# Gate modulation moved into block 0's attention, a third convolution tap per unit there, more on ScalarE, and 12 gate weights stored one block later

## The chip, the core and the metric

The kernel runs on one NeuronCore of a Trainium2 chip. Five engines have queues of their own: TensorE (PE in the profile; its weight loads are PEld), VectorE (DVE), ScalarE (ACT), GpSimd (POOL) and SyncE (SP, which here only issues DMAs). Each engine works through its queue in order. The metric is the device time of one execution in microseconds; lower is better.

## What is computed

One inference step of a streaming encoder layer, over 2048 prompt frames and 32 sample frames of width 1024, all in float32:

```python
mod = c @ w_mod + b_mod                       # shift, scale, gate: 3 x 1024
h = rms_norm(x, g_pre) * (1 + scale) + shift
z = h @ w_in                                  # 5632 columns: a b z_conv q k v z_attn g_conv g_attn
u = a * sigmoid(b)
y = causal_depthwise_conv(u, width 31) + dw_b
y_conv = (silu(layer_norm(y)) * silu(z_conv)) @ w_conv_out
o = band_attention(q, k, v, bias)             # own 64-frame chunk and the 8 before it, 8 heads
y_attn = (o * silu(z_attn)) @ w_attn_out
merged = sigmoid(g_conv) * y_conv + sigmoid(g_attn) * y_attn
y = x + gate * rms_norm(merged @ w_o, g_post)
```

## The kernel before

A float32 operand is split in two parts, `hi` (rounded to the matmul's float32r) and `lo` (the remainder); a product takes three matmuls, hi·hi, hi·lo and lo·hi (`mm3`). The work goes in four blocks of 512 prompt frames; block 0 also has the 32 sample frames, so its streams are 544 wide and its projections run as two matmuls of 272 columns where the other blocks run one of 512.

A block has these stages. The **attention**: the v projection, then 24 (block 0) or 16 units of scores, softmax, transposes and value products, with the projections of q, k, a, b, z between them as filler, in the order that `FILL` names. The **gate stage**: 16 gate projections (`C_GC`, `C_GA`; matmul tile `pj`, evacuated by ACT into `t`) with the attention branch's output product (`py<-ah`) after every fourth; a DVE instruction `t<-t,py` evacuates that. The **conv-out stage**: 8 steps of 24 matmuls `py<-cohi,w` and `py<-colo,w`, each step led by four transposes `pxt` of the next block's input, which `h_part` scales (`hh`, `hf`) and splits. Then the **output stage** with `w_o`, the post-norm and the stores.

The convolution is 31 taps for each of four channel tiles, 124 DVE instructions `y<-u,dww,y` a block. They are put between other work: in attention by `pace.pump(TP[i])` at three places in a unit, elsewhere wherever the planner `Pace`, which counts TensorE and VectorE time as it writes the program, finds DVE behind. When all taps are done, `norm_conv` follows (POOL sums, two means by matmul `pmean`, `rsqrt` on DVE) and then `co`, which makes `cohi` and `colo`; the conv-out stage needs all four channel tiles of them.

A weight of 0.5 MB is loaded by SP into one of two buffers `raw` (`w_load`, four weights ahead of its use), copied by ACT and subtracted by DVE or POOL into one of three buffers `w` (`w_parts`, two ahead); in block 0 ACT then issues a 1 MB store of both halves (`w_keep`, one ahead). Later blocks load the stored halves (`w<-kept`) and split nothing. In block 0's gate stage (`pace.dense`) every split is DVE's. The eight weights of the gate's modulation (`mod`) are used there too, in `gate_rows`: four pairs of four matmuls `pm` for each half of the row, then `pg`, two DVE instructions and a store of the row to DRAM.

Every engine's order but SP's is the order in which the program is written. Matmul results live in three PSUM tiles of the tag `pp` (`pj`, `py`, `pm`, `pg`, `pmean`, `pxt`): a new one waits until the engine that evacuates the third last is through.

## Time and profile before

| | |
|---|---|
| three timed runs | median 1776.56 us (1776.23 to 1776.82) |
| the profiled execution | 1774.66 us, of it span 1772.9 us |
| mean granted TensorE clock | 0.982 |
| PE busy | 1690.7 us (95%) |
| PEld busy | 1430.4 us (81%) |
| DVE busy | 1154.7 us (65%) |
| ACT busy | 597.5 us (34%) |
| POOL busy | 212.1 us (12%) |
| DMA | 368.61 MB, mean 208 GB/s |

The span is from the first instruction to the last; the profiled execution's own time has 1.76 us more around it. An engine that is busy all along can still be slow, and a busy share is a mean over stages with different limits, so the stages have to be read one by one. In the rows below, a time in brackets is how long the engine sat idle before the instruction, with the instruction that ended the wait.

### The profile page before, as it was taken

Reading aid. Unit: us, or ns where it says so; the run is one execution under the profiler, and the core shown is the slowest. Engines: PE = TensorE matmul, PEld = TensorE weight load, DVE = VectorE, ACT = ScalarE, POOL = GpSimd, SP = SyncE. Lnnn points to the kernel's source line nnn. Section 1 sums busy time; section 2 is a strip of 40 time slices with the busy share of each in tenths; the row PEclk is TensorE's granted clock in tenths of the full one; section 3 lists DMA queues with packets and bytes.
Section 4 is the critical chain, followed back from the end, with each engine's and each line's share of the span. In section 5 each row is a group of like instructions: output and inputs, shape, how many; then the busy total and the mean of one; then the engine's idle time right before and its main releaser. Section 6 shows DMA issues by size and latency. Waiting matters only on the chain.

```text
span 1772.9 us, 23618 instructions
## 1 busy us (share of the span) xinstructions
PE 1690.7 (95%) x9221; PEld 1430.4 (81%) x9221; DVE 1154.7 (65%) x2119; ACT 597.5 (34%) x1156; POOL 212.1 (12%) x163
## 2 busy tenths in 40 slices
PE   6889999989499999999899999999999999999997
PEld 4778899988388788888788888888888888888886
DVE  6556876887855957775652967765652967766523
ACT  5345454233331245531220035531320045531211
POOL 4322222002220000001120000001120000000120
PEclk9999999999699999999999999999999999999999
DMA  8796565767375684465465585455565574445553
GB/s 267 216 326 207 189 215 202 272 229 262 132 255 196 243 305 174 156 221 190 150 217 188 196 307 188 140 198 210 181 218 191 199 272 144 171 167 201 190 190 143
DMA packets 132326, 368.61 MB, mean 208 GB/s; under 512 B 9326, under 2 KB 75050, under 8 KB 101975
## 3 DMA queue, kind: packets, MB, share of 16 engines
q1 hardware_dynamic: 123575, 304.19, 50.1%
q10 hardware_dynamic: 8640, 62.92, 8.7%
q8 instruction: 73, 1.20, 0.3%
q14 instruction: 38, 0.31, 0.1%
HBM read 280.41 MB, written 91.77 MB: 210 GB/s over the span
## 4 chain that ended last, share of the span: by engine, by line
PE 78%; DVE 8%; DMA 4%; ACT 2%; issue 1%; ACTq 0%; POOL 0%; DVEq 0%; SPq 0%; POOLq 0%
PE pj L153 44%; PE py L153 8%; PE pv L153 4%; PE sps L153 4%; PE pt L157 4%; PE op L153 3%; PE oT L153 3%; PE oS L153 3%; PE oP L153 1%; DVE y L134 1%; DVE w L134 1%; PE vS L153 1%; PE vT L153 1%; DMA raw<-in_w_attn_out_dram 1%; DMA raw<-in_w_in_dram 1%
## 5 line engine op out<-in xcount | busy, mean ns | idle before, releaser
L153 PE MATMUL pj<-hh,w 128*128 128x512 f32 (+1 forms) x4800 | 974.7, 357 | 11.9 <-DVE kk L134 6.1
L153 PEld LDWEIGHTS pj<-hh,w 128*128 128x128 f32 x4800 | 778.4, 189 | 133.2 <-issue 8.9
L134 DVE SCALAR_TENSOR_TENSOR y<-u,dww,y 128x512 f32<-128x512 f32 (+1 forms) x480 | 338.2, 770 | 0.4
L1073 ACT ACTIVATE sp<-sp,mn 128x640 f32<-128x640 f32 (+5 forms) x136 | 103.7, 762 | 112.5 <-DVE mn L134 112.3
L1108 ACT ACTIVATE pth<-pt 128x256 fp32r<-128x256 f32 (+4 forms) x184 | 91.9, 501 | 135.8 <-PE pt L157 129.3
L134 DVE TENSOR_TENSOR ptl<-pt,pth 128x256 fp32r<-128x256 f32 (+4 forms) x184 | 104.2, 567 | 27.2 <-ACT pth L1108 25.4
L134 DVE CUSTOM_DVE_ANT_0 sp<-sps,bias 128x640 f32<-128x640 f32 (+4 forms) x128 | 94.4, 737 | 29.6 <-PE sps L153 28.1
L153 PE MATMUL py<-cohi,w 128*128 128x512 f32 (+1 forms) x320 | 93.5, 366 | 19.2 <-ACT cohi L1260 17.7
L226 ACT ACTIVATE w<-raw 128x1024 fp32r<-128x1024 f32 x72 | 75.6, 1054 | 89.1 <-DMA raw<-in_w_mod_dram 18.6
L153 PE MATMUL py<-ah,w 128*128 128x512 f32 (+1 forms) x480 | 96.3, 356 | 8.3 <-DVE t L134 7.1
L153 PEld LDWEIGHTS py<-ah,w 128*128 128x128 f32 x480 | 80.1, 192 | 23.5 <-DVE t L134 7.5
L157 PE MATMUL pt<-ident,sp 128*128 128x128 f32 (+1 forms) x600 | 94.2, 272 | 0.0
L228 POOL TENSOR_TENSOR w<-raw,w 128x1024 fp32r<-128x1024 f32 x30 | 73.3, 2443 | 170.5 <-ACT w L226 142.8
L528 POOL TENSOR_TENSOR u<-y 128x512 f32<-128x512 f32 (+1 forms) x4 | 6.3, 1581 | 671.4 <-DVE y L134 671.4
L153 PEld LDWEIGHTS py<-cohi,w 128*128 128x128 f32 x320 | 58.8, 195 | 29.0 <-ACT cohi L1260 19.1
L134 DVE TENSOR_SCALAR sp<-sp,ll 128x640 f32<-128x640 f32 (+5 forms) x136 | 75.6, 556 | 4.8
L134 DVE TENSOR_TENSOR w<-raw,w 128x1024 fp32r<-128x1024 f32 x42 | 53.3, 1278 | 31.5 <-ACT w L226 31.0
L153 PE MATMUL sps<-kk,qh 128*128 128x320 f32 (+1 forms) x224 | 69.2, 316 | 3.3 <-DVE kk L134 2.0
L157 PEld LDWEIGHTS pt<-ident,sp 128*128 128x128 f32 (+1 forms) x600 | 68.8, 140 | 3.9 <-issue 1.3
L153 PE MATMUL sps<-kk,ql 128*128 128x320 f32 (+1 forms) x224 | 70.8, 323 | 0.0
L1344 POOL TENSOR_TENSOR mg<-mg,t 128x512 f32<-128x512 f32 (+1 forms) x32 | 46.4, 1451 | 168.7 <-issue 114.0
L134 DVE SCALAR_TENSOR_TENSOR t<-t,py 128x512 f32<-128x512 f32 (+1 forms) x40 | 23.2, 584 | 59.3 <-PE py L153 59.2
(247 smaller groups left out, 2224.8 us busy)
## 6 DMA issues: line engine op xcount, KB each, us to landing
w<-kept SPq DMA_DIRECT2D x176, 1024.0 KB
kept<-w ACTq DMA_DIRECT2D x60, 1024.0 KB
raw<-in_w_in_dram SPq DMA_DIRECT2D x48, 512.0 KB
bias<-bias_d SPq DMA_DIRECT2D x32, 320.0 KB
xt<-in_x_prompt_dram SPq DMA_DIRECT2D x16, 512.0 KB
wm<-in_w_mod_dram SPq DMA_DIRECT2D x16, 512.0 KB
xr<-in_x_prompt_dram SPq DMA_DIRECT2D x16, 512.0 KB
vs_d<-vcur SPq DMA_DIRECT2D x12, 512.0 KB
```

The source lines that it names most:

```text
L134: return fn(out, *a, **k)
L153: nc.tensor.matmul(out, lhsT=lhsT, rhs=rhs, start=start, stop=stop)
L157: nc.tensor.transpose(out, in_, idn)
L226: act(wh, raw, AF.Copy)
L228: (V if on_v else G).tensor_tensor(wl, raw, wh.bitcast(F32), op=OP.subtract)
L528: G.tensor_tensor(s2[:, 0:YW], Y[2][:, 0:YW], Y[3][:, 0:YW], op=OP.add)
L1073: self.ex[i] = lambda: act(sp[0:m, 0:nk], sp[0:m, 0:nk], AF.Exp, bias=mn[0:m], scale=-1.0, accum_out=ll[0:m])
L1108: act(self.ph[0:r, f0:f1], pt[0:r, o:o + f1 - f0], AF.Copy)
L1344: G.tensor_tensor(mg, mg, t2, op=OP.add)
```

## The change

Seven edits:

1. The modulation's eight weights leave the gate stage. `FILL(0)` gets `m0` to `m7` between the projections of block 0's attention, and `mod_part` takes the place of `gate_rows`: each weight's four matmuls go into a `pp` tile of their own, and the partial sums are added in SBUF (two ACT copies, six DVE additions), in the space of `aof`. In attention the planner gives their split to POOL.
2. `TP` becomes (1, 1, 1): a third tap in each of 21 units of block 0's attention. The fill budget goes from 88 to 95 us.
3. `twice` names 12 gate weights (channels 256 to 1023 of both gates) beside v's: block 0 doesn't store them; block 1 loads them raw, splits them once more on DVE and stores them; blocks 2 and 3 load the halves as before.
4. In `h_part` and in `co`, the instructions `hf` and `xn<-y,vecs` go from DVE to ACT.
5. `rsqrt` has 9 instructions where it had 11 (one step of higher order in place of two), and the factor 1/1024 of the mean goes into the squares.
6. `ql`, which lies in the `raw` buffers, is made anew in blocks 2 and 3, with four POOL memsets each, since block 1 now loads into them.
7. A yield of 1.5 between `pg` and its DVE instructions.

```diff
-TP = (1, 1, 0)
+TP = (1, 1, 1)
...
-    order = "b0 a0 q1 k1 b1 a1 b2 q2 k2 a2 z0 b3 a3 z1 q3 k3 z2 z3 c0 c1 c2 c3" if b == 0 else \
+    order = "b0 a0 q1 m0 k1 m1 b1 m2 a1 m3 b2 q2 m4 k2 m5 a2 m6 z0 m7 b3 a3 z1 q3 k3 z2 z3 c0 c1 c2 c3" if b == 0 else \
...
-                if b == 0 and m + i:
-                    plan.append(mods.pop(0))
...
+    def twice(key):
+        return key[0] == "v" or key[0] == "in" and key[1] >= C_GC + 2 * P and not C_GA <= key[1] < C_GA + 2 * P
-    keep_at = {key: at[1 if key[0] == "v" else 0] for key, at in uses.items()}
+    keep_at = {key: at[1 if twice(key) else 0] for key, at in uses.items()}
...
-                on_v = key[0] == "mod" or pace.dense or pace.idle is None and pace.dve <= pace.pe + DV
+                on_v = pace.dense or key[0] == "in" and i > uses[key][0] or pace.idle is None and pace.dve <= pace.pe + DV
...
-        V.tensor_scalar(xh, x, -0.5, None, op0=OP.mult)
-        for _ in range(iters):
-            V.tensor_tensor(t, y, y, op=OP.mult)
-            V.tensor_tensor(t, t, xh, op=OP.mult)
-            V.scalar_tensor_tensor(y, t, 1.5, y, op0=OP.add, op1=OP.mult)
+        V.scalar_tensor_tensor(t, y, -0.5, y, op0=OP.mult, op1=OP.mult)
+        V.tensor_tensor(t, t, x, op=OP.mult)
+        V.scalar_tensor_tensor(y, t, 1.5, y, op0=OP.add, op1=OP.mult)
+        V.tensor_tensor(t, y, y, op=OP.mult)
+        V.tensor_tensor(t, t, x, op=OP.mult)
+        V.tensor_scalar(u, t, 0.375, -1.25, op0=OP.mult, op1=OP.add)
+        V.tensor_tensor(u, u, t, op=OP.mult)
+        V.scalar_tensor_tensor(y, u, 1.875, y, op0=OP.add, op1=OP.mult)
...
-        V.tensor_scalar(hf, src, Gm[:, w, ct:ct + 1], Sh[:, w, ct:ct + 1], op0=OP.mult, op1=OP.add)
+        act(hf, src, AF.Identity, scale=Gm[:, w, ct:ct + 1], bias=Sh[:, w, ct:ct + 1])
...
+    def mod_part(i):
+        n, kp = i // 4, i % 4
+        m4, bm, gr = aof[0:4, 3, 0:512], aof[0:2, 2, 0:512], aof[0:2, 1, 0:512]
+        if kp == 0:
             nc.sync.dma_start(bm, dram(b_mod, 2 * D + n * 512, [[0, 2], [1, 512]]))
             nc.sync.dma_start(gr, dram(g_post, n * 512, [[0, 2], [1, 512]]))
+        wh, wl = weights(("mod", 2 * kp, (4 + n) * 512))
+        pm = pp_tile("pm")
+        for kk in range(2):
+            mm(pm[0:4], c4[:, 2 * kp + kk, :], wh[:, kk, :], kk == 0, False)
+            mm(pm[0:4], c4[:, 2 * kp + kk, :], wl[:, kk, :], False, kk == 1)
+            yield
+        if kp == 0:
+            act(m4, pm[0:4], AF.Copy)
+        else:
+            V.tensor_tensor(m4, pm[0:4], m4, op=OP.add)
+        if kp == 3:
+            pace.start(gate_row(n, m4, bm, gr), 1.5)
...
-            if b == 1:
+            if b:
+                qls.clear()
...
-            rate = (88.0 if b == 0 else 62.0) / sum(loads)
+            rate = (95.0 if b == 0 else 62.0) / sum(loads)
...
-                        V.tensor_scalar(xn[ct][:, o0:o1], Y[ct][:, a0:a1], vecs[:, 44 + ct:45 + ct],
-                                        vecs[:, 48 + ct:49 + ct], op0=OP.mult, op1=OP.add)
+                        act(xn[ct][:, o0:o1], Y[ct][:, a0:a1], AF.Identity, scale=vecs[:, 44 + ct:45 + ct],
+                            bias=vecs[:, 48 + ct:49 + ct])
```

How the order moves shows at three places. TensorE, block 0, the last third of the gate stage up to the first conv-out step; `pmean` are the means of `norm_conv`, the second pair of rows of each group for the sample columns. Before:

```order
L153 MATMUL pj<-hh,w 128x272 x93
L153 MATMUL pmean<-lnhi,onesr 128x512
L153 MATMUL pmean<-lnlo,onesr 128x512
L153 MATMUL pmean<-lnhi,onesr 128x32
L153 MATMUL pmean<-lnlo,onesr 128x32
L153 MATMUL pj<-hh,w 128x272 x3
L153 MATMUL pm<-w,c_91 4x512 x4
L153 MATMUL py<-ah,w 128x272 x48
L153 MATMUL pm<-w,c_91 4x512 x4
L583 MATMUL pg<-m_4460,sel 2x512
```

After it came the second `pmean` group and then `pxt`. Now:

```order
L155 MATMUL pj<-hh,w 128x272 x45
L155 MATMUL pmean<-lnhi,onesr 128x512
L155 MATMUL pmean<-lnlo,onesr 128x512
L155 MATMUL pmean<-lnhi,onesr 128x32
L155 MATMUL pmean<-lnlo,onesr 128x32
L155 MATMUL pj<-hh,w 128x272 x147
L155 MATMUL py<-ah,w 128x272 x48
L159 MATMUL pxt<-ident,xt 128x128 x4
L155 MATMUL py<-cohi,w 128x272
```

This is the second group: 147 + 48 matmuls now stand between it and the conv-out stage where none stood, and no `pm` or `pg` is left here.

VectorE, block 0's attention, from one sample unit into the next unit (`ISA` are the bias and minimum of the scores, `ptl` the low half of the transposed softmax). Before:

```order
L134 TENSOR_SCALAR sp<-sp,ll 32x544
L134 SCALAR_TENSOR_TENSOR y<-u,dww,y 128x574
L134 TENSOR_TENSOR kk<-pj,kk 64x272 x4
L134 TENSOR_TENSOR vh<-zcb,vh 128x4x128
L134 ISA sp,mn<-sps,bias 128x128
L134 ISA mn 128x1
L134 TENSOR_TENSOR ptl<-pt,pth 128x512
```

Now:

```order
L136 TENSOR_SCALAR sp<-sp,ll 32x544
L136 SCALAR_TENSOR_TENSOR y<-u,dww,y 128x574
L136 TENSOR_TENSOR kk<-pj,kk 64x272 x4
L136 TENSOR_TENSOR vh<-zcb,vh 128x4x128
L136 SCALAR_TENSOR_TENSOR y<-u,dww,y 128x574
L136 TENSOR_TENSOR aof<-pm,aof 4x512
L136 ISA sp,mn<-sps,bias 128x128
L136 ISA mn 128x1
```

A tap and an addition of `pm` have come in ahead of the scores. Over the whole attention the taps go from 42 to 63, and those that are left for the gate stage from 82 to 61.

VectorE, block 1's gate stage, where `t<-t,py` evacuates the second product of the third `py` group (`ss`, `rr`, `rt`, `ru` belong to the statistics of the next block's input, `u` to `norm_conv`'s `rsqrt`). Before:

```order
L134 TENSOR_TENSOR ru<-rr 128x8
L134 TENSOR_TENSOR ru<-ru,rt 128x8
L134 SCALAR_TENSOR_TENSOR rr<-ru,rr 128x8
L134 TENSOR_SCALAR xt<-xt,rr 128x1024 x4
L134 SCALAR_TENSOR_TENSOR t_8066<-t_8066,py 128x512
L134 SCALAR_TENSOR_TENSOR t_8152<-t_8152,py 128x512
L134 TENSOR_SCALAR xn<-y,vecs 128x512
```

Ahead of these stood the 11 instructions on `u`, with no `t` between. Now:

```order
L136 TENSOR_SCALAR xt<-xt,rr 128x1024
L136 SCALAR_TENSOR_TENSOR t_8074<-t_8074,py 128x512
L136 TENSOR_SCALAR u<-pmean 128x512
L136 TENSOR_SCALAR u<-u 128x512
L136 SCALAR_TENSOR_TENSOR u<-u 128x512
L136 TENSOR_TENSOR u<-u 128x512
L136 SCALAR_TENSOR_TENSOR u<-u 128x512
L136 TENSOR_TENSOR u<-u 128x512 x2
L136 TENSOR_SCALAR u<-u 128x512
L136 TENSOR_TENSOR u<-u 128x512
L136 SCALAR_TENSOR_TENSOR u<-u 128x512
L136 SCALAR_TENSOR_TENSOR t_8164<-t_8164,py 128x512
```

The statistics and the `xt` now stand ahead of the first `t`, and only the shorter chain on `u` between the two. In the same stage 12 splits `w<-raw` have come into this queue.

## Rows read from the trace of the kernel before

**Rows 1.** Stretches: PE, PEld, DVE, ACT, POOL busy (instructions), PE clock, DMA share, GB/s.

```profile
120.00:300.00 180.00, 176.10 (x1329) 158.76 (x1328) 129.89 (x308) 90.38 (x217) 48.23 (x24) 1.00 0.58 203
300.00:450.00 150.00, 136.89 (x1009) 127.86 (x1009) 119.44 (x170) 50.03 (x79) 11.64 (x6) 0.96 0.73 253
450.00:504.00 54.00, 33.71 (x221) 30.45 (x222) 49.12 (x76) 21.82 (x38) 19.07 (x15) 0.76 0.43 150
...
775.00:895.00 120.00, 115.52 (x490) 93.14 (x489) 76.29 (x121) 25.29 (x43) 11.53 (x9) 0.97 0.56 202
```

**Rows 2.** PE in order of time, gate stage of block 0: start, us, instruction, [idle before].

```profile
344.84 1.09 PE L153 MATMUL pm<-w,c 128*4 128x512 f32 x4
345.77 12.16 PE L153 MATMUL pj<-hh,w 128*128 128x272 f32 x96
...
369.98 3.09 PE L153 MATMUL py<-ah,w 128*128 128x272 f32 x12 [6.22 <-DVE t L134]
...
404.29 1.01 PE L583 MATMUL pg<-m,sel 4*2 4x512 f32 x2 [1.54 <-DVE t L134]
...
435.91 6.25 PE L153 MATMUL py<-ah,w 128*128 128x272 f32 x48 [1.05 <-ACT t L1302]
...
445.16 1.46 PE L583 MATMUL pg<-m,sel 4*2 4x512 f32 x2 [2.07 <-DVE m L134]
```

**Rows 3.** The chain that ended last, in order of time: start, us, what.

```profile
359.20 7.97 DMA raw<-in_w_in_dram
...
369.58 0.36 DVE t L134
```

**Rows 4.** PE in order of time, conv-out stage of block 0.

```profile
447.85 1.11 PE L157 MATMUL pxt<-ident,xt 128*128 128x128 f32 x4
462.79 0.59 PE L153 MATMUL py<-cohi,w 128*128 128x272 f32 x1 [13.82 <-ACT cohi L1260]
...
476.25 0.64 PE L157 MATMUL pxt<-ident,xt 128*128 128x128 f32 x4
...
479.73 0.60 PE L157 MATMUL pxt<-ident,xt 128*128 128x128 f32 x4
...
484.04 0.66 PE L157 MATMUL pxt<-ident,xt 128*128 128x128 f32 x4 [0.71 <-DVE hf L134]
```

**Rows 5.** DVE and ACT in order of time, up to the first conv-out step.

```profile
462.64 1.10 ACT L1248 ACTIVATE th<-y,hg 128x512 f32<-128x512 f32 x2
...
472.13 0.73 DVE L134 SCALAR_TENSOR_TENSOR colo<-xn,cohi 128x544 fp32r<-128x544 f32 x1 [0.78 <-ACT cohi L1260]
```

**Rows 6.** Groups on DVE, 300 to 450 us: xcount | busy us, mean ns | idle before.

```profile
L134 DVE SCALAR_TENSOR_TENSOR y<-u,dww,y 128x574 f32<-128x574 f32 x80 | 60.8, 812 | 0.3
L134 DVE TENSOR_TENSOR w<-raw,w 128x1024 fp32r<-128x1024 f32 x28 | 35.3, 1270 | 24.9 <-ACT w L226 24.5 <-issue 0.4
L134 DVE TENSOR_TENSOR bg<-pg,bg 2x512 f32<-2x512 f32 x2 | 1.4, 678 | 0.9 <-PE pg L583 0.9
```

**Rows 7.** The same groups, 120 to 300 us.

```profile
L134 DVE SCALAR_TENSOR_TENSOR y<-u,dww,y 128x574 f32<-128x574 f32 x40 | 36.2, 906 | 0.1
```

**Rows 8.** All engines in order of time, one moment in block 0's attention.

```profile
214.31 3.05 DVE L134 SCALAR_TENSOR_TENSOR y<-u,dww,y 128x574 f32<-128x574 f32 x1
214.34 2.40 POOL L228 TENSOR_TENSOR w<-raw,w 128x1024 fp32r<-128x1024 f32 x1 [5.33 <-DMA raw<-in_w_in_dram]
```

**Rows 9.** All engines in order of time, gate stage of block 1, PE's rows.

```profile
817.65 8.09 PE L153 MATMUL pj<-hh,w 128*128 128x512 f32 x34
...
870.11 19.57 PE L153 MATMUL pj<-hh,w 128*128 128x512 f32 x72 [4.48 <-DVE t L134]
```

**Rows 10.** All engines in order of time, the beginning and block 0's first projections.

```profile
51.03 1.86 PE L670 MATMUL pc<-sel,m 4*128 4x2 f32 x8 [4.61 <-DVE m L134]
...
97.54 3.60 PE L153 MATMUL pj<-hh,w 128*128 128x272 f32 x15 [6.06 <-DVE kk L134]
```

**Rows 11.** PE in order of time, the first weights of block 1.

```profile
614.39 1.42 PE L153 MATMUL vS<-w,hh 128*128 128x512 f32 x5 [2.58 <-DVE w L134]
```

More of the change, by code (lines that the diff above doesn't have):

```diff
@@ L35 @@
 NIN = 5632
+C_MOD = -1
 BIG = 1e30
@@ L52, in FILL @@
 def FILL(b):
-    part = dict(q=C_Q, k=C_K, a=C_A, b=C_B, z=C_ZA, c=C_ZC)
-    order = "b0 a0 q1 k1 b1 a1 b2 q2 k2 a2 z0 b3 a3 z1 q3 k3 z2 z3 c0 c1 c2 c3" if b == 0 else \
+    part = dict(q=C_Q, k=C_K, a=C_A, b=C_B, z=C_ZA, c=C_ZC, m=C_MOD)
+    order = "b0 a0 q1 m0 k1 m1 b1 m2 a1 m3 b2 q2 m4 k2 m5 a2 m6 z0 m7 b3 a3 z1 q3 k3 z2 z3 c0 c1 c2 c3" if b == 0 else \
         "q1 k1 z0 q2 k2 z1 q3 k3 z2 z3 c0 c1 c2 c3"
@@ L182, in w_half, with w_fill @@
         return ((name, m), 2 * P, lambda r: (r, src[0, :, m * P:(m + 2) * P].rearrange("(k p) c -> p k c", p=P)))
-    mods = [w_wide("mod", w_mod, k, n * 512) for n in (4, 5) for k in range(0, KT, 2)]
+    def w_fill(n, col):
+        return w_wide("mod", w_mod, 2 * (n % 4), (4 + n // 4) * 512) if col == C_MOD else w_cols(col + n * P)
     for b in range(NB):
         plan += [w_wide("v", w_in, k, C_V) for k in range(0, KT, 2)]
-        plan += [w_cols(c + n * P) for n, c in [(0, C_Q), (0, C_K)] + FILL(b)]
+        plan += [w_fill(n, c) for n, c in [(0, C_Q), (0, C_K)] + FILL(b)]
         for m in range(0, KT, 2):
@@ L586, in gate_row @@
         nc.sync.dma_start(gp_d[:, n * 512:(n + 1) * 512], bm)
+        gate_done.add(n)
         yield 0.0
@@ L941, in sink @@
                 def sink(o, c0, c1):
+                    assert len(gate_done) == 2 or key == ("za", 0)
                     tz = tmp("tz")
@@ L1293, in mixer_kernel @@
             xs = []
-            gr = gate_rows(lambda name: tl_.tile([P, D], F32, tag="x", name=name, bufs=XB)) if b == 0 else None
             for m2 in range(0, KT, 2):
@@ L1302, in mixer_kernel @@
                     pace.run(proj(C_GA + m * P, b, lambda o, c0, c1: act(t2[:, c0:c1], o, AF.Tanh, scale=0.5)))
-                    if gr and m:
-                        for i in range(2):
-                            next(gr, None)
-                            pace.tick()
                 wa = weights(("ao", m2))
@@ L1311, in mixer_kernel @@
                         t2[:, c0:c1], t2[:, c0:c1], 1.0, o, op0=OP.add, op1=OP.mult)))
-            if gr:
-                for _ in gr:
-                    pace.tick()
             while pace.idle is not None:
```

38 lines of the change are left out of this document (11 added, 27 removed).

## The prediction

> **What bounds the kernel now.** I read the shares of the engines first: TensorE is busy 1690.7 of 1772.9 us, so at most some 82 us of waiting can be won, plus what a lowered clock costs. Then I cut the span into stretches, to see where that waiting sits [rows 1]. Block 0's attention has 176.1 of 180 us busy at a granted clock of 1.00. Its gate stage has 136.9 of 150 at 0.96, the 54 us after it only 33.7 at 0.76 (between the two levels, 1.2 and 2.4 GHz), and block 1's gate stage 115.5 of 120 at 0.97. So the time to be won lies mostly between 300 and 504 us, and there TensorE waits for other engines. The rest is TensorE's own work, and no edit takes any of that away. Third came TensorE's order of time with what ended each wait.
>
> Between the stages stands the longest wait, 13.82 us: the first product with `cohi` waits for the chain from the second `pmean` through `rsqrt` and `co` [rows 4]. From the `pxt` at 447.85 to the next step's at 476.25 go 28.40 us, while the next step takes 476.25 to 479.73, 3.48. The difference, 24.9 us, is waiting and the half clock that the first products run at afterwards.
>
> In the gate stage four waits come to 6.22 + 1.54 + 1.05 + 2.07 = 10.9 us [rows 2]. Products after them are slow: 12 take 3.09 us where 96 of the same width take 12.16 (126.7 ns each), which makes 1.6 too much, and the second `pg` pair takes 1.46 for 1.01. So the gate stage loses some 12.9 us. The longest wait is read from the chain: a raw weight needed 7.97 us to land, and the split that it feeds stands in VectorE's queue ahead of `t`, for which TensorE waits [rows 3]. VectorE splits 28 weights here, 1270 ns each, and stands idle 24.5 us for their ACT copies, 0.87 each [rows 6].
>
> **Block 0's conv-out stage (edits 1, 2, 4, 5).** The second `pmean` group moves ahead: 147 + 48 matmuls now stand between it and `cohi`, 195 x 126.7 ns = 24.7 us, to which the 1.1 us of `pxt` come. The chain that they hide took from 447.85 to the last `colo` at 472.86, 25.0 us [rows 4, 5]. It loses two instructions of `rsqrt` (0.73 each, taken from the `colo` of that width, together 1.5) and has five splits put into it (5 x 1.27 = 6.4): 29.9. Against 25.8 of cover some 4 us stay open; `xn` leaving VectorE takes perhaps 1 from it. I take 3 left and a gain of 22. Bounds: everything hidden, 24.9; or ACT's `xn` comes on the path four times at about 1.1 (the nearest row is `th`, two instructions in 1.10) and the five splits wait 0.87 each, 8.8 more left, a gain of 12 to 13. What is late next is the third `py` group, since its `t` stands behind the same chain; that is in the lower end.
>
> **Block 0's gate stage (1, 2, 3).** Of VectorE's queue there go 8 splits of `mod` (10.2 us and 7 of waiting) and 21 taps of 812 ns (17.1) [rows 6]. Of the queue of transfers there go 8 raw loads of 0.5 MB and 12 stores of 1 MB, 16 of the 150 x 253 = 38 MB that were moved there [rows 1]. What made the 7.97 us of landing is so mostly gone, and both `pg` waits go by construction. Gain 11 of 12.9. Bounds: the late weight stays with its slow products (6.22 + 1.57), leaving 5; or all, 13. The moved matmuls themselves are worth nothing: eight fours of `pm` at 0.93 (344.84 to 345.77) and two `pg` of 1.0 leave this stage, 9.5 us, and return in the attention.
>
> **Conv-out steps (4).** With `hf` on ACT the waits for `hf` change engine. There are four in this stage, the first 0.71 [rows 4], together 2.2. `hf` now stands behind `hh` on ACT, so part of it may come back. Gain 1 (0 to 2.2).
>
> **Attention of block 0 (1, 2).** VectorE gets 21 taps x 906 ns [rows 7] = 19.0, six additions of `pm` at 0.68 (the nearest row is `bg<-pg,bg`, [rows 6]) = 4.1, and four instructions of `gate_row` = 2.7: 25.8 us. It was busy 129.9 of 180; it becomes 155.7 of 189.5, 82% instead of 72. POOL gets eight splits of 2.40 [rows 8], 19 on 48 [rows 1]. TensorE waited 3.9 us here at 72%. Nothing is hidden for certain, since the scores' minimum and `ptl` stand in that queue behind the taps. But 18% stays free, and TensorE has filler products ahead. I take a second 4 us, so a loss of 4; bounds 0 and the whole 26, if each added instruction lands on the path.
>
> The profile shows that POOL can hold VectorE: one tap took 3.05 us while a split ran on POOL for 2.40 [rows 8]. But the mean of 40 taps is 906 ns here and 812 in the gate stage, 94 x 40 = 3.8 us in all. The Trainium skill (SBUF — State Buffer, section "Who interferes with whom") says of the port pair that both engines share that an instruction holds it to its end and the other one blocks, and that VectorE with two SBUF inputs contends with GpSimd's reads. By that rule it would be up to 19 us for the added splits; the trace agrees for the single tap and not for the mean.
>
> **Block 1 (3, 4, 5).** Its gate stage waits 4.48 us for a `t` behind the `u` chain, and 72 matmuls after it take 19.57 us, 272 ns each, where 34 before took 8.09, 238 each [rows 9]: 2.4 more, 6.9 in all. After the change the statistics stand ahead of the first `t`, and the `u` chain is two shorter. Against it come 12 splits, 15.2 us on 76.3 of 120 [rows 1], and the loads: 12 raw weights and 12 stores in place of 12 loads of halves, 6 MB more. I take a gain of 5. Bounds: 7, and below nothing a loss of 6.2 if one raw weight comes as late as in block 0 [rows 2].
>
> **The rest.** At the beginning the wait of 4.61 us at 51.03 is for VectorE, which `hf` and two `rsqrt` instructions leave: gain 2 (4.6, or a loss of 1 if ACT is late). The wait of 6.06 for `kk` at 97.54 [rows 10] hangs on one transfer queue, whose order shifts when 12 stores fall out: gain 1.5 (3, or a loss of 2). The wait of 2.58 at 614.39 [rows 11] and the end hang on the same short `rsqrt`: two instructions fewer of under 0.68 us each, 0.4 taken for each place, 0.8.
>
> **The sum.** -22 - 11 + 0 - 1 + 4 - 5 - 2 - 1.5 - 0.8 = -39.3 us. The profiled execution took 1774.66 us, so 1735.4; it was 1.9 below the median of 1776.56, so 1737.3.
>
> **Rivals.**
> A. The attention has no room: all 25.8 us of VectorE's new work land on the path. For it: VectorE feeds the softmax in order. Against it: TensorE idled only 3.9 us of 180. 22 more than taken: 1759.
> B. Slower. Each `pm` piece takes one of three `pp` tiles, and that is free only when the addition is reached in VectorE's queue; projections behind it wait. The price is the only wait of this kind in the trace, 6.06 for `kk` [rows 10]: 8 x 6.06 = 48.5 in place of 4, 1737.3 + 44.5 = 1782. It decides from 43.3 / 8 = 5.4 us a piece. Against it: the other filler projections go through the same queue with nearly no wait.
> C. The change doesn't do what it says for the transfers: the gate stage's weights stay late with fewer bytes, and block 1, which gets the raw loads and stores, shows the same once. 11 + 5 are not won and 6.2 come on top: 1759.
> D. POOL's eight added splits hold VectorE over their whole length in the attention, as in the one tap of [rows 8]: 8 x 2.40 = 19 in place of 4: 1753. The Trainium skill's rule on the shared port pair, named above, would give just this.
>
> **Chances and range.** Forecast 0.68, A 0.11, C 0.08, D 0.08, B 0.05. The low end takes the better bounds of the large terms (2.9 of the conv-out wait, 2 each of the gate stages, 4 of the attention, 4 of the beginning): 1722. The high end covers D and the middle of A and C: 1760. Left out are B and the outer parts of A, C and the forecast, under 2 in 10. Differences under 0.2% (3.6 us) are about what a measurement of this kernel can't tell from none. Only B is slower (0.05); A or C with poor bounds elsewhere may fall to no change (0.03); the rest, 0.92, is faster.
>
> **What the profile after would show.** The conv-out wait: first `cohi` product right behind `pxt` with under 4 us idle, and a clock near 1.00 there. The gate stage: no wait of over 2 us, `raw` landing well below 7.97. The attention: VectorE some 156 us busy and TensorE idle about 8 in 190; 26 idle would be A, a long wait ahead of projections behind `pm` B, taps of 1.2 us mean D. Block 1: no 4.48 wait and matmuls near 238 ns, else C. I am wrong above all if TensorE's idle time turns up again in the attention.

## The result: the time and the profile after

The changed kernel takes 1755.79 us (median of four runs, 1754.62 to 1756.64), the kernel before 1776.69 beside it. The ratio is 0.9879, 95% interval 0.9862 to 0.9896: 1.2% faster, 20.9 us. The forecast was 1737.3, 39 us faster. The time lies inside the range, the direction is right, and the gain is half of what the sum gave. That it lies inside is owed to the room that the range left for the rivals A, C and D, and to misses that partly cancel: the attention came out 28 us worse than the sum had it and the gate stage 5, the start 6, the first conv-out step 3 and block 1 with what follows 4 better.

One sentence ahead of the prediction has to be put right first: in the kernel before, the `pm` of the gate's modulation did not lie in a `pp` tile but in one of two tiles of another tag, `T`. Only the changed kernel puts `pm` into `pp`. That matters below.

Cut at the same events, the profiled executions compare so (us; "first scores" is when TensorE begins the attention, a stage runs to the first instruction of the next, the first conv-out step is from its `pxt` to the next step's):

| | before | after | difference | forecast |
|---|---|---|---|---|
| start to first scores | 101.0 | 91.7 | -9.3 | -3.5 |
| attention of block 0, to the first `py<-ah` | 224.3 | 265.8 | +41.5, of it 9.5 moved in | +4 besides the 9.5 |
| gate stage of block 0 | 122.6 | 106.8 | -15.8, of it 9.5 moved out | -11 besides the 9.5 |
| first conv-out step | 28.4 | 3.5 | -24.9 | -22 |
| conv-out steps to the wait in block 1's v | 138.1 | 136.9 | -1.3 | -1.4 |
| from there to the end | 1158.5 | 1149.5 | -9.1 | -5.4 |
| span | 1772.9 | 1754.1 | -18.8 | -39.3 |

All terms but the attention's and the gate stage's came out as forecast or better. The attention lost 32 us where 4 were forecast. Its rows and the ones that answer [rows 1], from the stretches of the changed kernel (columns as there):

```profile
91.70:357.50 265.80, 241.57 (x1692) 211.38 (x1691) 195.36 (x396) 116.37 (x265) 78.88 (x35) 0.94 0.64 220
...
245.00:357.50 112.50, 111.33 (x865) 103.95 (x864) 86.14 (x169) 50.37 (x114) 28.43 (x12) 1.00 0.64 226
...
357.50:464.30 106.80, 100.22 (x778) 98.99 (x777) 85.28 (x126) 43.49 (x75) 17.02 (x14) 0.98 0.39 131
464.30:467.77 3.47, 3.47 (x30) 3.47 (x29) 2.48 (x4) 2.40 (x3) 0.00 (x0) 1.00 1.00 394
...
755.00:875.00 120.00, 120.00 (x537) 97.90 (x536) 89.83 (x131) 42.99 (x67) 13.95 (x9) 1.00 0.73 258
```

In the attention TensorE is idle for 24.2 us, and its clock is 0.94; the same stretch of the kernel before has

```profile
101.00:325.30 224.30, 220.31 (x1659) 200.08 (x1658) 160.12 (x365) 108.10 (x256) 54.18 (x26) 1.00 0.64 222
```

so 20 of the 32 us are waiting, and 12 are busy time at a lowered clock (241.6 against 220.3 + 9.5). The second row says where: from 245 us on, when the last `pm` and `pg` are through (237 us), TensorE is busy 111.3 of 112.5 us at 1.00, with three taps in all but the last units. The loss lies ahead of that, in the part that has a late weight at its start and then the modulation in it.

The conv-out stage and block 1 answer [rows 2], [rows 4] and [rows 9] in TensorE's order of time:

```profile
364.84 3.09 PE L155 MATMUL py<-ah,w 128*128 128x272 f32 x12 [2.70 <-DVE t L136]
...
459.37 1.76 PE L155 MATMUL py<-ah,w 128*128 128x272 f32 x12 [1.10 <-ACT t L1313]
462.72 1.76 PE L155 MATMUL py<-ah,w 128*128 128x272 f32 x12 [1.59 <-DVE t L136]
464.32 0.60 PE L159 MATMUL pxt<-ident,xt 128*128 128x128 f32 x4
467.77 0.60 PE L159 MATMUL pxt<-ident,xt 128*128 128x128 f32 x4
...
871.37 5.75 PE L155 MATMUL py<-ah,w 128*128 128x512 f32 x24
```

The 13.82 us ahead of the first `cohi` product are gone without a rest, and block 1's wait of 4.48 too. In the gate stage 2.70 us and the slow 3.09 behind it stay. The chain shows the same cause as [rows 3], with a raw weight that landed still later:

```profile
351.40 10.64 DMA raw<-in_w_in_dram
...
363.21 1.23 DVE w L136
364.44 0.36 DVE t L136
```

The longest of TensorE's waits in the attention end with VectorE. Three of the moments, all engines in order of time, with what stands around them:

```profile
98.08 1.06 ACT L229 ACTIVATE w<-raw 128x1024 fp32r<-128x1024 f32 x1 [6.49 <-DMA raw<-in_w_in_dram]
...
99.21 2.34 POOL L231 TENSOR_TENSOR w<-raw,w 128x1024 fp32r<-128x1024 f32 x1 [9.48 <-ACT w L229]
...
99.75 1.88 DVE L136 TENSOR_SCALAR sp<-sp,ll 128x128 f32<-128x128 f32 x1
...
102.03 0.69 PE L155 MATMUL sps<-kk,qh 128*128 128x384 f32 x1 [5.88 <-DVE mn L136]
...
137.41 1.09 PE L155 MATMUL pm<-w,c 128*4 128x512 f32 x4
...
139.70 1.04 ACT L229 ACTIVATE w<-raw 128x1024 fp32r<-128x1024 f32 x1
...
140.65 0.37 ACT L865 ACTIVATE kk<-pj 64x272 fp32r<-64x272 f32 x1
...
141.50 1.81 DVE L136 TENSOR_TENSOR kk<-pj,kk 64x272 fp32r<-64x272 f32 x4
...
142.54 1.41 PE L155 MATMUL pj<-hh,w 128*128 128x272 f32 x6 [4.03 <-DVE kk L136]
...
144.01 2.46 POOL L231 TENSOR_TENSOR w<-raw,w 128x1024 fp32r<-128x1024 f32 x1 [0.30 <-POOL w L231]
144.17 2.91 DVE L136 SCALAR_TENSOR_TENSOR y<-u,dww,y 128x574 f32<-128x574 f32 x1
...
230.51 5.16 POOL L231 TENSOR_TENSOR w<-raw,w 128x1024 fp32r<-128x1024 f32 x2 [4.23 <-ACT w L229]
...
233.40 2.89 DVE L136 SCALAR_TENSOR_TENSOR y<-u,dww,y 128x574 f32<-128x574 f32 x1
236.21 0.67 DVE L136 TENSOR_TENSOR aof<-pm,aof 4x512 f32<-4x512 f32 x1
...
236.94 1.86 PE L590 MATMUL pg<-aof,sel 4*2 4x512 f32 x2 [3.46 <-DVE aof L136]
238.53 0.29 DVE L136 TENSOR_SCALAR sp<-sp,ll 128x128 f32<-128x128 f32 x1
```

The first is the place to which the gain at the start went. Attention begins 9.3 us earlier, but a raw weight is not there until 98 us; ACT stands 6.49 us at its copy, with the exponentials (`sp<-sp,mn`) of the first scores queued behind it, and VectorE and TensorE behind those. The kernel before waited for `kk` up to nearly the same time (97.54, [rows 10]). In the second, a `pm` stands ahead of the projection that waits. ACT copies a weight before it comes to `kk` (140.65), and VectorE's half of `kk` ends the wait; the tap of 2.91 us, beside a split on POOL, comes only after it. In the third, a tap of 2.89 us, beside two splits on POOL, and the last addition of a half row (236.21) stand in VectorE's queue ahead of what `pg` reads.

So there are four suspects for the 26 us that the attention lost beyond the late weight: the third tap; the eight splits on POOL; the weights' loads and copies; and the pieces themselves, with their additions on VectorE and their `pp` tiles.

### The profile page after: what moved, and what is told of

It is laid out like the page before. It is cut to its first block, busy times and chain, and to the rows that moved or that the text cites. A ratio compares the mean times of both kernels' runs of the same rounds, so it can differ in the third digit from the quotient of the medians.

```text
span 1754.1 us, 23638 instructions
## 1 busy us (share of the span) xinstructions
PE 1690.4 (96%) x9221; PEld 1432.0 (82%) x9221; DVE 1135.1 (65%) x2042; ACT 645.4 (37%) x1230; POOL 237.7 (14%) x178
## 4 chain that ended last, share of the span: by engine, by line
PE 85%; DVE 7%; ACT 3%; DMA 3%; issue 1%; POOL 0%; SPq 0%; ACTq 0%; POOLq 0%; DVEq 0%
PE pj L155 47%; PE py L155 9%; PE pv L155 4%; PE sps L155 4%; PE pt L159 4%; PE op L155 3%; PE oT L155 3%; PE oS L155 3%; PE vS L155 2%; PE vT L155 2%; DVE sp L136 2%; PE oP L155 1%; DMA raw<-in_w_in_dram 1%; DVE y L136 1%; DMA wm<-in_w_mod_dram 1%
## 5 line engine op out<-in xcount | busy, mean ns | idle before, releaser
L155 PE MATMUL pj<-hh,w 128*128 128x512 f32 (+1 forms) x4800 | 977.7, 358 | 10.4 <-DVE kk L136 4.0
L136 DVE SCALAR_TENSOR_TENSOR y<-u,dww,y 128x512 f32<-128x512 f32 (+1 forms) x480 | 345.8, 781 | 0.5
L136 DVE TENSOR_TENSOR ptl<-pt,pth 128x256 fp32r<-128x256 f32 (+4 forms) x184 | 104.1, 566 | 30.2 <-ACT pth L1120 28.7
L229 ACT ACTIVATE w<-raw 128x1024 fp32r<-128x1024 f32 x84 | 88.3, 1053 | 82.0 <-PE py L155 29.0
L231 POOL TENSOR_TENSOR w<-raw,w 128x1024 fp32r<-128x1024 f32 x37 | 92.1, 2495 | 194.4 <-ACT w L229 170.5
L136 DVE CUSTOM_DVE_ANT_0 sp<-sps,bias 128x640 f32<-128x640 f32 (+4 forms) x128 | 94.1, 735 | 29.5 <-PE sps L155 28.4
L159 PE MATMUL pt<-ident,sp 128*128 128x128 f32 (+1 forms) x600 | 95.2, 274 | 0.0
L136 DVE TENSOR_SCALAR sp<-sp,ll 128x640 f32<-128x640 f32 (+5 forms) x136 | 84.6, 622 | 4.8
L136 DVE TENSOR_TENSOR w<-raw,w 128x1024 fp32r<-128x1024 f32 x47 | 60.9, 1299 | 35.9 <-ACT w L229 35.3
L1348 POOL TENSOR_TENSOR mg<-mg,t 128x512 f32<-128x512 f32 (+1 forms) x32 | 46.4, 1450 | 159.3 <-issue 105.9
L1312 ACT ACTIVATE t<-pj 128x512 f32<-128x512 f32 (+1 forms) x40 | 20.7, 517 | 125.5 <-PE pj L155 125.4
```

The source lines that it names most:

```text
L136: return fn(out, *a, **k)
L155: nc.tensor.matmul(out, lhsT=lhsT, rhs=rhs, start=start, stop=stop)
L159: nc.tensor.transpose(out, in_, idn)
L229: act(wh, raw, AF.Copy)
L231: (V if on_v else G).tensor_tensor(wl, raw, wh.bitcast(F32), op=OP.subtract)
L1312: pace.run(proj(C_GC + m * P, b, lambda o, c0, c1: act(t1[:, c0:c1], o, AF.Tanh, scale=0.5)))
```

## The experiments

The runs were made on two chips, on which the kernel before took 1775.7 and 1776.2 (1776.7 beside the changed kernel). Stretches come from each run's one profile. The attention and gate stage are cut as above, and VectorE's busy time is that in the attention.

One cut more is needed. The attention begins with the late raw weight just described, and that weight landed at another time in each profile: at 93.1 us in "mod not split", at 94.3 in "no mod weights", at 95.2 to 98.7 in the other runs that waited for it. TensorE's wait for it, up to 6.2 us, is in the attention whatever the edit was. So the column "behind the late weight" starts at the first scores of the sample frames (`sa`), which come after that wait, and ends with the attention. How far single profiles differ can be read from two pairs of runs whose attention has the same work: "after" and "edit 3 undone" lie 4.0 us apart in the attention and 1.8 behind the weight, "edit 1 undone" with and without edit 3 1.8 and 1.7. A difference of under 2 us in that column says nothing.

| kernel | median | first scores | attention | behind the late weight | DVE busy in it | gate stage | first conv-out step |
|---|---|---|---|---|---|---|---|
| before | 1776 | 101.0 | 224.3 | 215.4 | 160.1 | 122.6 | 28.4 |
| third tap alone | 1763.7 | 103.9 | 227.9 | 218.1 | 175.3 | 128.2 | 3.9 |
| edit 1 alone | 1778.5 | 97.0 | 250.0 | 241.0 | 176.8 | 104.1 | 28.3 |
| after | 1755.8 | 91.7 | 265.8 | 247.9 | 195.4 | 106.8 | 3.5 |
| after, edit 1 undone | 1739.5 | 95.7 | 233.3 | 220.2 | 178.2 | 116.4 | 3.5 |
| the same, budget 88 | 1742.0 | 92.7 | 233.4 | 220.7 | 177.2 | 119.7 | 3.5 |
| the same as two above, edit 3 undone too | 1754.2 | 90.7 | 235.1 | 218.5 | 178.7 | 128.1 | 3.6 |
| after, two taps | 1766.3 | 93.2 | 253.7 | 237.8 | 178.9 | 102.5 | 26.4 |
| after, edit 3 undone | 1757.6 | 91.1 | 261.8 | 246.1 | 194.9 | 106.8 | 3.5 |
| after, mod split on DVE | 1768.0 | 91.7 | 272.4 | 251.3 | 198.2 | 110.2 | 3.6 |
| after, mod not split | 1750.9 | 90.5 | 259.3 | 246.6 | 187.7 | 107.0 | 3.5 |
| after, no mod weights | 1747.1 | 93.2 | 255.8 | 246.0 | 188.5 | 107.3 | 3.4 |
| the same, two tiles and six additions | 1742.7 | 91.2 | 250.7 | 234.4 | 185.0 | 105.9 | 3.5 |
| the same, two tiles, no additions | 1736.7 | 91.8 | 245.0 | 228.6 | 179.1 | 106.6 | 3.5 |

**Edit 1 undone.** Is it the modulation or the tap?

```diff
-    order = "b0 a0 q1 m0 k1 m1 b1 m2 a1 m3 b2 q2 m4 k2 m5 a2 m6 z0 m7 b3 a3 ...
+    order = "b0 a0 q1 k1 b1 a1 b2 q2 k2 a2 z0 b3 a3 ...
...
+                if b == 0 and m + i:
+                    plan.append(mods.pop(0))
```

(and `gate_rows` back in the gate stage.) Expected:

> The changed kernel with edit 1 undone: the modulation's eight weights are used in block 0's gate stage again, all other edits stay (three taps a unit in attention, rate 95, 12 gate weights split twice, hf and xn on ACT, the short rsqrt). In the changed kernel (1755.8 us) TensorE's attention stretch from its first scores to the first py takes 265.8 us against 224.3 before, and 9.5 of that is moved work: 32 too much. Theory M (the modulation's pieces cause it): about 23 of the 32 go away, some 6 to 9 stay, which came in with a late raw weight at 98 us; attention near 233 us; the gate stage takes back 9.5 us of matmuls and some 5 to 10 us of waits, so 1738 to 1750. Theory T (the third tap loads VectorE): the attention stays at 250 to 256 us, and the gate stage is worse all the same: 1760 to 1770.

Measured: 1739.5 us (1738.7 to 1741.0), ratio to before 0.9792, interval 0.9777 to 0.9807. It is 16 us faster than the changed kernel and the fastest kernel here that computes the whole: the modulation is better left where it was. The attention takes 233.3 us, as theory M had it. The surprise is the gate stage: it takes back the 9.5 us of matmuls and nothing more (116.4 against 106.8), where 5 to 10 us of waits were expected with them. So, with edit 3 in place, edit 1 had won no waiting there.

**Two taps.**

```diff
-TP = (1, 1, 1)
+TP = (1, 1, 0)
```

> The changed kernel with two taps a unit in block 0's attention in place of three, nothing else. Theory T: the attention stretch loses 20 us or more (265.8 to 245), and the tail pays up to 17 for 21 taps of 0.81 us, so 1745 to 1760. Theory M: the attention stretch changes by under 5 us, and the tail pays for the taps, since the second pmean group falls back: 1758 to 1772.

Measured: 1766.3 us (1765.7 to 1769.9), 10.5 slower than with three. Both theories were half right: the attention gets 12 us shorter (10 behind the late weight), but the second `pmean` group comes last again and the wait before the conv-out stage is back. TensorE's order in this run:

```profile
448.71 0.39 PE L155 MATMUL pmean<-lnhi,onesr 128*128 128x512 f32 x1
...
449.40 0.66 PE L159 MATMUL pxt<-ident,xt 128*128 128x128 f32 x4
462.84 0.59 PE L155 MATMUL py<-cohi,w 128*128 128x272 f32 x1 [12.79 <-ACT cohi L1272]
...
475.75 0.76 PE L159 MATMUL pxt<-ident,xt 128*128 128x128 f32 x4
```

**The third tap alone**, in the kernel before (the same line there, from 0 to 1):

> The kernel before with the third tap a unit in block 0's attention alone (edit 2 without the larger budget). If the third tap is what brings the second pmean group forward: of the 24.9 us before the conv-out stage 20 to 25 go, the attention pays 5 to 9: 1757 to 1764. If it takes the short rsqrt, xn on ACT or the modulation out of the tail as well: 10 or less go, 1768 to 1778.

Measured: 1763.7 us (1762.9 to 1765.8), ratio 0.9934, interval 0.9917 to 0.9950. The first conv-out step falls from 28.4 to 3.9 us: the tap alone does what the prediction ascribed to edits 1, 2, 4 and 5 together. In the attention it costs 3.6 us without the modulation (2.7 behind the late weight), against 12 (10) with it, in the run above. The rest of the gain is lost at the start, 2.9 us later, and in the gate stage, 5.7 us longer: the `co` chain now stands in it, among weights that are as late as in the kernel before (ACT waits 36 us for raw weights in that stage in either).

**Edit 1 alone**, in the kernel before:

> The kernel before with edit 1 alone (the modulation's weights in block 0's attention, the fill budget at 95 for them, edit 7's yield); two taps, old rsqrt, hf and xn on VectorE, all gate weights stored in block 0. Theory M from the earlier runs (the pieces cost 23 us in the attention besides the 9.5 that move): the attention, 224.3 us before, becomes 250 to 260; the gate stage gives back 9.5 and 5 to 10 us of waits; the 24.9 us before the conv-out stage stay, since the second pmean group is as late as before: 1780 to 1792, slower than before. If the cost appears only together with the third tap: 1768 to 1777.

Measured: 1778.5 us (1773.4 to 1786.0, ten runs), ratio 1.0018, interval 1.0004 to 1.0032; by its interval a little slower, by the 0.2% that a measurement can tell no change. The time lies between the two ranges; the attention is 250.0 us as theory M had it, 16 us too much (241.0 behind the late weight, also 16). So the modulation costs without the third tap too. The gate stage gives back 18.5: 9.5 of moved matmuls, 6.3 of waiting, and the rest by the clock, 1.00 in place of 0.96. Edit 1 does shorten the gate stage where nothing else has, and pays more for it elsewhere.

**What in the modulation costs.** First without its splits (the low part is left out, the high part read twice):

```diff
-                (V if on_v else G).tensor_tensor(wl, raw, wh.bitcast(F32), op=OP.subtract)
+                if key[0] != "mod":
+                    (V if on_v else G).tensor_tensor(wl, raw, wh.bitcast(F32), op=OP.subtract)
...
-            mm(pm[0:4], c4[:, 2 * kp + kk, :], wl[:, kk, :], False, kk == 1)
+            mm(pm[0:4], c4[:, 2 * kp + kk, :], wh[:, kk, :], False, kk == 1)
```

> The changed kernel without the eight splits of the modulation's weights on POOL: they are loaded and copied by ACT as before, but the low part isn't made and the matmuls read the high part twice (that part of the gate is left out). Theory M-P (the splits on POOL hold VectorE's instructions): of some 23 us that the modulation costs in the attention 12 to 20 go: 1736 to 1744. Theory M-S (the weights come too fast one after the other, raw loads are late and hold ACT's queue) or M-Q (the pieces themselves: pp tiles, additions and pg in the queues): under 5 us, 1751 to 1757.

Measured: 1750.9 us (1750.1 to 1752.7), 4.9 less: at the edge of what M-S and M-Q had, far from M-P. Eight splits of 2.5 us on POOL cost a quarter of their length, not the whole. The profile does not even show that much: the attention is 6.5 us shorter, but only 1.3 of it lies behind the late weight, which landed 5 us earlier here.

VectorE does get its instructions through faster: the same 396 of them take 187.7 us in place of 195.4. Which ones were held can be read from the groups (count, busy us, mean ns, idle before), in the changed kernel

```profile
L136 DVE SCALAR_TENSOR_TENSOR y<-u,dww,y 128x574 f32<-128x574 f32 x74 | 69.0, 944 | 0.2
L136 DVE TENSOR_SCALAR sp<-sp,ll 128x384 f32<-128x384 f32 x8 | 8.8, 1100 | 0.3
L136 DVE TENSOR_TENSOR kk<-pj,kk 64x272 fp32r<-64x272 f32 x14 | 6.1, 438 | 2.1 <-ACT kk L866 1.8
```

and without the splits

```profile
L136 DVE SCALAR_TENSOR_TENSOR y<-u,dww,y 128x574 f32<-128x574 f32 x74 | 66.9, 916 | 0.2
L136 DVE TENSOR_SCALAR sp<-sp,ll 128x384 f32<-128x384 f32 x8 | 5.4, 671 | 0.3
L136 DVE TENSOR_TENSOR kk<-pj,kk 64x272 fp32r<-64x272 f32 x14 | 6.1, 439 | 2.1 <-ACT kk L867 1.8
```

The taps and `sp<-sp,ll` 128x384, which read SBUF alone, get shorter on the mean; `kk<-pj,kk`, which reads a matmul's result, does not, nor does the bias of the scores (`sp<-sps,bias` 128x512: 684 and 686 ns). So eight splits held VectorE for 7.7 us in all, of which 1.3 (behind the late weight) to 4.9 (the medians) reached the time.

Then the eight splits on VectorE instead:

```diff
-                on_v = pace.dense or ...
+                on_v = key[0] == "mod" or pace.dense or ...
```

> The changed kernel with the eight splits of the modulation's weights on VectorE in place of POOL. Without them it took 1750.9, 4.9 less than with them on POOL. Theory P (POOL's splits hold VectorE for their length): VectorE pays 8 x 1.27 = 10 us of its own for up to 19 us of holds: 1748 to 1754. Theory V (VectorE is what the attention waits for, and any work in its queue costs): 1756 to 1766.

Measured: 1768.0 us (1766.2 to 1769.2), 12.2 slower than with them on POOL, as theory V had it. The attention has 6.6 of that, 3.4 of it behind the late weight, and the gate stage 3.4. It is not the splits' length alone: VectorE also stands still in the attention for 11.1 us until ACT has copied a weight (6.2 at the modulation's first), where in the changed kernel that is 3.5. So a split costs more in VectorE's queue than on POOL, by its work and by what it waits for; the two were not taken apart.

Then without the weights (matmuls on columns of `hh`; neither load, copy nor split):

```diff
-        plan += [w_fill(n, c) for n, c in [(0, C_Q), (0, C_K)] + FILL(b)]
+        plan += [w_fill(n, c) for n, c in [(0, C_Q), (0, C_K)] + FILL(b) if c != C_MOD]
...
-        wh, wl = weights(("mod", 2 * kp, (4 + n) * 512))
...
-            mm(pm[0:4], c4[:, 2 * kp + kk, :], wh[:, kk, :], kk == 0, False)
-            mm(pm[0:4], c4[:, 2 * kp + kk, :], wl[:, kk, :], False, kk == 1)
+            mm(pm[0:4], c4[:, 2 * kp + kk, :], hh[:, kk, 0, 0:512], kk == 0, False)
+            mm(pm[0:4], c4[:, 2 * kp + kk, :], hh[:, kk, 0, 0:512], False, kk == 1)
```

> The changed kernel in which the modulation's matmuls read columns of hh in place of weights: its eight weights are neither loaded nor copied nor split (the gate's modulation is left out), the pm matmuls, the additions and pg stay. Theory M-P: the same as without the splits, within 4 us. Theory M-S: 15 to 23 us less than the changed kernel (1733 to 1741) while the run without splits gains under 5. Theory M-Q: under 5 us less, 1751 to 1757.

Measured: 1747.1 us (1743.6 to 1748.9), 8.6 less than the changed kernel and 3.8 less than without the splits. None of the three theories alone. By the medians the loads and copies are 3.8 us; behind the late weight, which was early here too, nothing is seen of them (246.6 and 246.0). The largest part stays with no weight at all: 246.0 against the 229.7 that the run with edit 1 undone gives with the moved 9.5 us.

Then each half row's sixteen matmuls in one tile, without the six additions:

```diff
+        if kp < 3:
+            yield
+            return
         pm = pp_tile("pm")
-        for kk in range(2):
+        for k in range(KT):
...
-        if kp == 0:
-            act(m4, pm[0:4], AF.Copy)
-        else:
-            V.tensor_tensor(m4, pm[0:4], m4, op=OP.add)
+        act(m4, pm[0:4], AF.Copy)
```

> As the run without the modulation's weights (1747.1 us; that part of the gate is left out here too), but the sixteen matmuls of each half row go into one pp tile, at the place of its fourth piece: two tiles in place of eight, no additions on VectorE, the same 32 matmuls and the same two pg. In the run without weights the attention stretch is 255.8 us, in the run with the modulation back in the gate stage 233.3, of the 22.5 between them 9.5 are the moved matmuls; 13 are open. Theory Q1 (each piece takes one of three pp tiles in turn and holds it until its addition is reached in VectorE's queue, for 1 us of work where a projection half brings 3): the stretch falls to 243 to 248, the time to 1734 to 1740. Theory Q2 (it is the matmuls and pg themselves, or filler moved by them): the stretch stays at 251 to 256, 1743 to 1749.

Measured: 1736.7 us (1734.6 to 1738.3): within Q1's range, 10.4 us less. But the edit does three things: it takes two tiles in place of eight, leaves out the additions, and lets the matmuls stand at two places in place of eight. The stretch of the run without weights, and of this one:

```profile
93.20:349.00 255.80, 238.89 (x1692) 210.71 (x1691) 188.45 (x396) 109.00 (x257) 58.14 (x27) 0.95 0.60 209
```

```profile
91.80:336.80 245.00, 234.20 (x1691) 206.88 (x1690) 179.14 (x390) 108.94 (x257) 58.09 (x27) 0.97 0.63 222
```

The matmuls are the same (1692 and 1691 records); TensorE waits 6 us less and is busy 4.7 us less, at a higher clock. And last, six additions of the same size put back, with no tile behind them:

```diff
+        if kp:
+            hq = hh[0:4, kp, 0, 0:512].bitcast(F32)
+            V.tensor_tensor(aof[0:4, 3, 0:512], hq, hq, op=OP.add)
```

> The run with two pm tiles in place of eight (1736.7 us, modulation's weights left out), and six additions of 512 columns on VectorE put back at the places of the pieces, on other data and with no matmul tile behind them. If the tiles of the pieces cost the 10 us: within 2 us of it, 1735 to 1739. If the additions in VectorE's queue do: 1741 to 1747.

Measured: 1742.7 us (1740.0 to 1743.4): the additions' side. Six instructions of some 0.68 us, 4.1 in all, cost 6.0 us by the medians, 5.7 in the attention and 5.8 behind the late weight. The other 4.4 (5.1 and 11.6) stay with the six tiles more, with the places of their matmuls, and with additions that wait for a matmul; these were not taken apart. Of TensorE's waits behind the late weight, those that end with an addition or another instruction on `aof` by VectorE come to 6.1 us in the changed kernel, 3.2 in the run without weights, and none with two tiles.

**The stores.** Edit 3 undone in the changed kernel:

```diff
-        return key[0] == "v" or key[0] == "in" and key[1] >= C_GC + 2 * P and not C_GA <= key[1] < C_GA + 2 * P
+        return key[0] == "v"
```

> The changed kernel with edit 3 undone for the gate weights: block 0 stores all 16 of them again, block 1 loads the halves and splits none. If the stores were what made block 0's raw weights late: its gate stage (106.8 us from the first py to the first pxt, of it 6.6 idle) gets 4 to 8 us longer, block 1 gains 0 to 2: 1758 to 1763. If the relief came from the other edits: 1753 to 1757.

Measured: 1757.6 us (1754.0 to 1762.3), not to be told from the changed kernel by runs that spread so far. The profile is clearer: block 0's gate stage is 106.8 us in both, with 249 GB/s moved in place of 131; in block 1 a wait of 2.38 us for `t` is back. And the same with the modulation in the gate stage:

> The kernel with the modulation back in the gate stage (1739.5 us) and edit 3 undone as well: block 0 stores all gate weights, block 1 splits none. With the modulation in attention the same undoing brought a wait of 2.4 us for a t back in block 1 and left block 0's gate stage at 106.8 us. Here the modulation's eight raw loads compete with the stores in the gate stage: if that is what made the raw weight late before, a wait of some 6 us comes back there, 1745 to 1750; else only block 1's: 1740 to 1744.

Measured: 1754.2 us (1753.8 to 1756.7), 14.7 slower than with edit 3, more than either side had. The gate stage is 128.1 us in place of 116.4. What ACT waited for at its copies there (time in total, times, longest) shows why, in this run

```profile
ACT w L234 <- DMA raw<-in_w_mod_dram: 21.4, 4, 7.7
ACT w L234 <- DMA raw<-in_w_in_dram: 7.4, 2, 5.3
ACT w L234 <- DMA raw<-in_w_attn_out_dram: 5.6, 2, 3.3
```

with edit 3 and the modulation back

```profile
ACT w L234 <- DMA raw<-in_w_mod_dram: 14.6, 3, 5.0
ACT w L234 <- DMA raw<-in_w_in_dram: 1.5, 1, 1.5
```

and in the changed kernel with edit 3 undone

```profile
ACT w L229 <- DMA raw<-in_w_in_dram: 3.9, 1, 3.9
```

ACT waits 34 us for raw weights where both the modulation's weights and the stores are in the stage, 16 without the stores, 4 without the modulation, with or without the stores. A weight of the modulation is used up in 1 us of TensorE's time, so the next is soon wanted; only together with the stores did that make the stage late.

**The budget.** The kernel with the modulation back, at 88 us of filler:

```diff
-            rate = (95.0 if b == 0 else 62.0) / sum(loads)
+            rate = (88.0 if b == 0 else 62.0) / sum(loads)
```

> The kernel with the modulation back in the gate stage (1739.5 us) and the fill budget at 88 us as before, since no modulation has to be filled in: its attention stretch took 233.3 us where the kernel before took 224.3. If the budget of 95 spends the filler too early, 3 to 6 us of the 9 go: 1733 to 1737. If the third tap makes them, no change: 1738 to 1742.

Measured: 1742.0 us (1737.3 to 1744.9): no gain, and the attention is 233.4 us as with 95. The budget is not what the 9 us over the kernel before are spent on. First scores and attention together are 325.3 us before and 329.0 and 326.1 in the two runs: the earlier start is given back at the late weight, and behind it the attention is 5 us longer than before in both (220.2 and 220.7 against 215.4), with the third tap in it.

## Why the prediction was right, and half wrong

**What bounds the kernel, and the conv-out wait: right.** The 24.9 us were where the rows had them, and behind the 195 matmuls nothing of the chain is left open; the gain was the upper bound, where the sum had left 3 us. The step ascribed it to edits 1, 2, 4 and 5. The run with the third tap alone shows that edit 2 does it by itself, by bringing the second `pmean` forward.

**Gate stage, 11 forecast: size wrong, cause double counted.** It gave 6.2 beside the moved matmuls: 10.64 us for one raw weight and the slow products behind it stay, as the lower bound had allowed. The step added the relief of edit 1 (eight loads less) and of edit 3 (twelve stores less). Four of the runs have three taps and all other edits, and in them the stage takes 128.1 us with neither, 116.4 with edit 3 alone, 106.8 with edit 1 alone and 106.8 with both. So each wins some 12 us beside the moved matmuls, but only without the other; with edit 1 in place edit 3 wins nothing in block 0.

The weight that stayed late was not helped by what the stage moves less (ACT waits 4 us for it with and without edit 3), as its load begins in the attention. Two stretches of the changed kernel, during the load and behind it:

```profile
351.40:362.00 10.60, 10.60 (x86) 10.52 (x85) 10.60 (x13) 2.14 (x4) 3.07 (x1) 1.00 1.01 356
362.00:375.00 13.00, 10.30 (x71) 10.16 (x70) 11.94 (x18) 3.40 (x5) 0.00 (x0) 0.87 0.29 85
```

The DMA engines were busy throughout up to 362 us, and the weight before this one took 9.53 us there as well. In the kernel before, the late weight took 7.97 us at 240 GB/s, so a full DMA is not the only thing that delays one.

**Attention, +4 forecast: the step that failed.** Measured +32. The step took TensorE's idle time of before (3.9 us at VectorE's 72%) and doubled it for 82%: it priced VectorE's new work by how much of that engine stays free. The runs show that this does not set the price. Behind the late weight, in the kernel before, with the third tap alone, with edit 1 alone, and in the changed kernel:

```profile
109.86:325.30 215.44, 211.45 (x1601) 192.55 (x1599) 156.32 (x351) 105.72 (x249) 52.17 (x25) 1.00 0.63 218
...
113.68:331.80 218.12, 211.54 (x1602) 192.59 (x1600) 171.70 (x371) 104.53 (x249) 55.92 (x26) 1.00 0.61 214
...
106.03:347.00 240.97, 225.68 (x1633) 199.46 (x1631) 172.97 (x361) 113.83 (x257) 72.80 (x33) 0.98 0.64 222
...
109.62:357.50 247.88, 229.52 (x1634) 201.54 (x1632) 188.88 (x379) 113.00 (x257) 76.54 (x34) 0.96 0.61 210
```

The tap makes VectorE 15.4 us busier and costs 2.7. Edit 1 makes it 16.7 busier and costs 16.1 beside the moved matmuls. Together they cost 23.0, 4 more than apart. The other 9.0 of the 32 lie ahead of the late weight's end: the earlier start, given back. VectorE's time was mis-sized as well: it got 35.2 us more in the attention (195.4 for 160.1) where 25.8 were forecast, and 7.7 of them are the holds by POOL's splits, which the step had left out.

What the modulation's 23 us in the attention (265.8 to 233.3, less 9.5) are made of is known only in part. The additions on VectorE make some 6, by the medians, the attention and the column behind the late weight alike. The eight tiles, with what goes with them, make 4.4 by the medians, 5.1 by the attention and 11.6 behind the late weight. The splits on POOL make 4.9, 6.5 and 1.3, and the loads and copies 3.8, 3.5 and 0.6. The cuts disagree since each is a difference of two single profiles, and since two of these had the late weight early. So the pieces themselves, the additions and what stands around them, are 10 to 17 us and the largest part; whether splits and weights cost 2 us or 9 stays open. With two taps, in the run of edit 1 alone, the modulation costs 16 by either cut; with three it is 23 by the attention and 18 behind the late weight.

A third of the loss is the clock, which the step did not price: 12 of the 32 us are matmuls at a granted clock of 0.94. Two of the stretches of the changed kernel:

```profile
124.90:145.00 20.10, 14.67 (x96) 11.70 (x94) 17.07 (x34) 12.06 (x26) 8.66 (x4) 0.95 0.60 190
...
225.00:245.00 20.00, 14.73 (x87) 11.04 (x86) 14.84 (x31) 5.39 (x13) 5.99 (x3) 0.83 0.59 200
```

Each has some 5.3 us of idle time; in the second, with the wait of 3.46 for `pg` in it, the clock lies well between the levels of 1.2 and 2.4 GHz.

**The rivals.** A came nearest: its price was 26 us in the attention and its time 1759, where 32 and 1755.8 were measured. In part that is luck: 9 of the 32 are the start given back, which A does not have. Its mechanism, all of VectorE's added work on the path, fits edit 1 (16.7 us of work, 16.1 of time) and not the tap (15.4 and 2.7). B was priced at 6.06 us a piece. All six tiles more are worth 4 to 12 us together, so under 2 a piece, far from its deciding point; that it is the holding of the tile was argued and not shown apart from where the matmuls stand. C came true in block 0 for one weight, which was later than before, and is refuted in block 1, whose gate stage has no wait left. D had the splits on POOL at 19 us; without them 4.9 go.

On D the rule was that of the Trainium skill (SBUF — State Buffer, section "Who interferes with whom"): GpSimd and VectorE share a port pair, and an instruction that holds it makes the other wait. The rows agree for single instructions: a `sp<-sp,ll` of 128x128 took 1.88 us while POOL split and 0.29 at 238.53 without, a tap 2.91. But eight splits, 19.7 us in all, made VectorE's instructions 7.7 us longer and the kernel 4.9 slower, so here the rule gives a bound from above and not the cost. The instructions that read a matmul's result kept their length beside the splits, as the groups above show.

**Start and block 1: right in sign, mechanism only in part.** The first scores came 9.3 us earlier where 3.5 were forecast, and 5.88 of that turned up as the next wait, a few us later. The step priced the waits of 4.61 and 6.06 without asking what is late next: the raw weight. Edit 1 alone starts 4 us earlier too, so what moved the start was not taken apart. Block 1 and the rest gave 9.1 for 5.4; there the 12 splits and loads cost nothing that can be seen, and the wait of 2.38 that comes back without edit 3 was not foreseen as its gain. Edits 4 and 5 were not run by themselves; how much of the 9.1 is theirs stays open.

## What to carry to other kernels

The free share of the engine that feeds the bottleneck does not price new work on it. Here nearly the same added time on VectorE cost 2.7 us as convolution taps and 16 with the pieces of a small product and their weights; so ask of each added instruction who waits behind it in that queue, and add the clock that the new gaps cost. When two edits relieve the same wait, price each with the other already in place: here either moved weights or dropped stores cleared the gate stage, and the one that was paid for cost 16 us more than it won. A small matmul in a rotating set of result tiles takes a slot as a large one does, so what its evacuation waits for belongs into its price. And parts of a few us can be read from single profiles only when it is known how far two profiles of the same work differ: here one late weight moved the stretch by 2 to 5 us.
